# Queries moved into the stage of seven block products, with attention's operands passed through DRAM

## The chip, the cores and the metric

The kernel runs on one core of a Trainium2 chip. The metric is the device time of one execution in microseconds (us). A core has five engines with a queue of instructions each, which they work off in order: PE (TensorE, matmuls), DVE (VectorE), ACT (ScalarE), POOL (GpSimd) and SP (SyncE, which here only issues DMAs).

## What is computed

One layer of a hybrid streaming encoder on a stream of 16 meta tokens and 1024 frames, model width 1024, all in float32. Cut to the part around the change:

```python
h = h + 0.5 * swiglu(rmsnorm(h, ffn1_norm), ...)
u = rmsnorm(h, mix_norm)
(aq, ak, av, gq, gk, gv, gr, g_low, gate_a, gate_b) = split(u @ w_in)
ya = window_sink_attention(aq, ak, av, att_sinks)   # 8 heads of 64, 2 key heads, chunks of 64, 2 chunks back
yb = rmsnorm(gated_linear_attention(gq, gk, gv, log_sigmoid(g_low @ gla_gate_w + gla_gate_b) / 16)) * silu(gr)
h = h + (sigmoid(gate_a) * (ya @ w_branch_att) + sigmoid(gate_b) * (yb @ w_branch_gla)) @ w_out
h = h + 0.5 * swiglu(rmsnorm(h, ffn2_norm), ...)
return rmsnorm(h, final_norm)[:, 16:]
```

`aq` is 512 columns wide, `ak` and `av` 128 each, `gq` and `gk` 256 each, `gv` and `gr` 512 each, the two gates 1024 each.

## The kernel before

A float32 product is made from three reduced-precision ones: each operand is split into a high part (a cast, by ACT) and a low part (a subtraction, by DVE), and PE adds high × high, low × high and high × low. So 128 output columns over all of a 1024-row contraction and 512 frames are 8 × 3 = 24 matmuls, and over 1024 frames 48.

The projections `u @ w_in` are made in two forms. The plain form (`mm`, lines 96 to 98, tile `pj`) takes those 48 matmuls for each block of 128 columns; its weights come by one load (`raw`), one ACT cast (`whi`, L125) and one DVE subtraction (`wlo`, L126). The other form (`Group`, `product`, line 454) takes a pair of blocks of 128 columns and the two halves of the frames as a 2 × 2 block matrix, and makes it with seven block products of 12 matmuls instead of eight: 84 for a pair, where the plain form has 96. Its operands are sums and differences of weight blocks (`s`, L437, split into `wop` by L228 and L229). Four outputs come out of products 1, 4, 5 and 6 of a pair, each 128 × 512 (`gate_evac`).

In order of the program:

1. After the first feed-forward layer, `together` (tiles `pj` at L929, L930 and after) projects two blocks of `gk`, two of `gq` and the first of `gr` in the plain form, with the norm's scales made meanwhile.
2. The stage of seven products: the loop at L1104 over the 16 blocks of the two gates, in 8 pairs. The last four pairs also carry `decay`, the gate math of the linear attention, in ACT, DVE and SP. In this loop the order of PE, ACT and DVE is the order of the code; elsewhere a scheduler sets it.
3. Plain projections for the attention: `ak`, `av` and the four blocks of `aq` (`project_units`, a list of units, one for each chunk of frames: 512, 256 and 272 columns for those with meta tokens, `CH_T`, and two of 512 for those without, `CH_FR`). Their outputs are copied from PSUM into the layouts that the attention reads: keys, high parts in two tiles `kh`, low in `kl`; values `vcat`; queries `qs`, in two tiles that hold the high part of one key head beside the low part of it. `kh`, `kl` and `vcat` have 8 blocks of 16 meta columns, 2 zero columns and 128 frames. `build_bias`, on POOL, makes the table `bias` for the scores (L1164 to L1189), after the zero columns (L1160). Eight loads bring back the second half of the frames of four tiles of `u` (`uh`, `ul` from `b12_dram`).
4. The attention, 16 rounds (L1400): `turn` transposes the probabilities p of a chunk (`tp`), `scores` makes those of the next chunk (`sp`; softmax on DVE and ACT: the maximum `mx`, exps at L1299, reciprocal L1300, scaling L1302), `values` transposes a block of `vcat` (`vt`) and splits it into `vz`, and then PE runs what the round's entry of `slots` holds before `attend` multiplies p with the values (`po`). The slots are the projections of `gv` (L1348, two entries a block: the 512 chunk, then both others), of `gr` (L1351, six entries) and in the last two rounds two fill units each, parts of `ya @ w_branch_att` times the gate (`ga`, L1384). Two query units are held back and run after the first scores (L1398).
5. The remaining 12 fill units, the linear attention, `w_out`, the second feed-forward layer.

The stores of projected blocks of `gv` go out after a transposition one unit later (`late`, L903 to L912): PE transposes, DVE copies (`g`), SP stores.

The names of buffers are reused: `raw`, `whi` and `wlo` are the weights of any plain unit; a tile pool that is closed (`g7.close()`, L1120) gives its memory to later tiles, whose first writer then waits for the last reader of the old ones.

Of the kernel before, what the change touches and what calls it, by code (L numbers as in the profile page):

```python
# [8 lines left out]
F32 = mybir.dt.float32  # L9
# [26 lines left out]
def hybrid_kernel(  # L36
# [779 lines left out]
    plain_views = [cols_view(w_in, c) for c in (C_GK, C_GK + P, C_GQ, C_GQ + P, C_GR)]  # L816
# [64 lines left out]
    gr_dram = dram.tile([4, P, S], F32, name="gr_dram")  # L881
    b12_dram = dram.tile([4, 2, P, 512], F32, name="b12_dram")
# [6 lines left out]
    def ev_keep(dst, scale=None):  # L889
        def evac(ps, c0, n):  # L890
            g = ttile("g")
            nc.scalar.activation(g[:, 0:n], ps[:, 0:n], AF.Copy, scale=1.0 if scale is None else scale)
            nc.sync.dma_start(out=dst[:, c0:c0 + n], in_=g[:, 0:n])
        return evac

    def ev_tok(i):

        def evac(ps, c0, n):
# [4 lines left out]
            def turn():  # L903
# [3 lines left out]
                if c0 + n == T:  # L907
# [9 lines left out]
    plain_evac = [ev_keep(gk_dram[0]), ev_keep(gk_dram[1]), ev_keep(gq_dram[0], 0.125), ev_keep(gq_dram[1], 0.125),  # L917
                  ev_keep(gr_dram[0])]
# [53 lines left out]
    together([(2, CH_FR[1]), (3, CH_FR[1])])  # L972
# [38 lines left out]
    def gate_weights(m):  # L1011

        pair = []
        for i in range(2):
            pair.append(g8.ext_tile() if m % 4 else raw_tile())
            c = C_GA + (m + i) * P
            nc.sync.dma_start(out=pair[-1].rearrange("p (k m) -> p k m", k=KT),
                              in_=w_in[:, c:c + P].rearrange("(k p) m -> p k m", p=P))
        return Group(g8, *pair)

    def gate_out(m, i, c, x):
        if m < KT:
            nc.scalar.activation(x, x, AF.Sigmoid)
        nc.sync.dma_start(out=gates[m + i, :, c * 512:(c + 1) * 512], in_=x)
# [74 lines left out]
    group, follow = gate_weights(0), gate_weights(2)  # L1099
# [4 lines left out]
    for m in range(0, 16, 2):  # L1104
        others = [decay(*x) for x in pieces.pop(0)] if m >= KT else []
# [12 lines left out]
        group, follow = follow, gate_weights(m + 4) if m + 4 < 16 else None  # L1118
# [72 lines left out]
    def ev_k(ps, c0, n):  # L1191
        fr, p0 = min(n, S - c0) // P, c0 // P
        parts = [(lambda t, p: blocks(t)[p, p0:p0 + fr, MB:KB], lambda p: ps[p, 0:fr * P].rearrange("p (a b) -> p a b", b=P))]
        if c0 + n == T:
            parts.append((lambda t, p: blocks(t)[p, :, 0:NM], lambda p: ps[p, n - NM:n].unsqueeze(1).to_broadcast([p.stop - p.start, 8, NM])))
        lo_, hi_ = slice(0, 64), slice(64, P)
# [582 lines left out]
```

## Time and profile before

| | |
|---|---|
| time, median of 3 runs | 2018.44 us (2017.83 to 2019.83) |
| profiled execution: own time, span | 2016.82 us, 2015.1 us |
| granted PE clock | 0.997 |
| matmuls | 12060 |

Times inside the profile count from the start of the span. Stage 2 runs from 777.6 to 932.1, stage 3 from there to 1000, the attention's rounds to about 1140, and the remaining fill units and the linear attention to about 1235. In a row of groups the columns are line, engine, operation, tile written and tiles read, shapes, count, busy time, mean duration in ns, and the engine's idle time before these instructions with what ended it. In a row of a timeline they are start, duration, engine, line, operation, tiles, shapes, count, and in brackets the idle time before it and what ended it.

### The profile page before, as it was taken

To read this page: it belongs to the slowest core of one execution; us is meant where nothing else is said; L and a number is where in the kernel's file an instruction comes from. 1 tells how busy PE (TensorE), PEld (TensorE's weight loads), DVE (VectorE), ACT (ScalarE), POOL (GpSimd) and SP (SyncE) were. 2 spreads that over 40 slices of the span, in tenths; PEclk is the share of its full clock that TensorE was granted. 3 is DMA by queue.
4 is the path that set the end of the run, shared out by engine and by line. 5 is a ranking of instruction groups with operands and counts; after the bars stand their busy time and mean duration, and the time that the engine had idled before them with its cause. 6 is when DMAs were issued, how large, how long until landed. Compare 5 with 4: busy or idle time off the path is not lost.

```text
span 2015.1 us, 32030 instructions
## 1 busy us (share of the span) xinstructions
PE 1989.4 (99%) x12060; PEld 1767.3 (88%) x12060; DVE 1408.7 (70%) x2451; ACT 886.5 (44%) x1728; POOL 187.9 (9%) x223
## 2 busy tenths in 40 slices
PE   8999999999999999999999999999999999999998
PEld 7999999999999988888898768888888888878888
DVE  6976776675778785566466568469767767758875
ACT  5544444443322354465366445345444444442222
POOL 1000000002322000005000000110000000023212
PEclk9999999999999999999999999999999999999999
DMA  6243443349975343355212746741534534699722
GB/s 212 85 148 127 160 169 127 127 161 377 358 280 190 100 132 102 105 178 173 63 51 61 239 139 210 230 149 48 183 126 155 180 126 147 209 384 347 276 89 84
DMA packets 284619, 343.05 MB, mean 170 GB/s; under 512 B 26406, under 2 KB 192032, under 8 KB 284464
## 3 DMA queue, kind: packets, MB, share of 16 engines
q1 hardware_dynamic: 265376, 274.82, 41.2%
q10 hardware_dynamic: 17296, 61.29, 8.0%
q0 software_dynamic: 1792, 4.89, 0.7%
q8 instruction: 95, 1.56, 0.3%
q14 instruction: 60, 0.49, 0.1%
HBM read 220.66 MB, written 120.27 MB: 169 GB/s over the span
## 4 chain that ended last, share of the span: by engine, by line
PE 88%; DMA 5%; DVE 3%; issue 1%; ACT 1%; POOL 0%; SPq 0%; DVEq 0%; ACTq 0%; POOLq 0%
PE pb L454 35%; PE pd L454 17%; PE pa L454 9%; PE pj L96 2%; PE pj L97 2%; PE pj L98 2%; PE wo L96 1%; PE wo L97 1%; PE wo L98 1%; PE pd L841 1%; DMA tm<-f2mid 1%; PE pj L929 1%; PE pj L930 1%; PE pj L931 1%; DMA tm<-f1mid 1%
## 5 line engine op out<-in xcount | busy, mean ns | idle before, releaser
L454 PE MATMUL pb<-tt,wop 128*128 128x260 f32 (+1 forms) x2280 | 393.0, 326 | 0.0
L454 PEld LDWEIGHTS pb<-tt,wop 128*128 128x128 f32 x2280 | 339.8, 188 | 35.5
L229 DVE TENSOR_TENSOR wop<-s,wop 128x512 fp32r<-128x512 f32 x268 | 190.6, 714 | 119.6 <-ACT wop L228 119.1
L228 ACT CAST wop<-s 128x512 fp32r<-128x512 f32 x268 | 166.1, 621 | 234.2 <-PE pb L454 90.5
L454 PE MATMUL pb<-tm,wop 128*128 128x260 f32 (+1 forms) x1440 | 235.9, 319 | 5.5 <-ACT h L396 3.4
L454 PEld LDWEIGHTS pb<-tm,wop 128*128 128x128 f32 x1440 | 208.2, 189 | 25.3 <-ACT h L396 4.1
L228 ACT CAST wop<-raw 128x512 fp32r<-128x512 f32 x201 | 124.8, 622 | 221.6 <-PE pb L454 110.8
L229 DVE TENSOR_TENSOR wop<-raw,wop 128x512 fp32r<-128x512 f32 x201 | 144.7, 721 | 29.7 <-ACT wop L228 29.5
L454 PE MATMUL pd<-tt,wop 128*128 128x260 f32 (+1 forms) x792 | 138.2, 327 | 0.0
L454 PEld LDWEIGHTS pd<-tt,wop 128*128 128x128 f32 x792 | 118.9, 188 | 13.1
L454 PE MATMUL pd<-tm,wop 128*128 128x260 f32 (+1 forms) x720 | 119.1, 319 | 0.0
L341 DVE SCALAR_TENSOR_TENSOR h<-pb,h 128x520 f32<-128x520 f32 (+1 forms) x136 | 93.4, 692 | 36.5 <-PE pb L454 34.7
L454 PE MATMUL pb<-tb,wop 128*128 128x260 f32 (+1 forms) x696 | 115.3, 319 | 0.7 <-DVE m L742 0.7
L454 PE MATMUL pd<-tb,wop 128*128 128x260 f32 (+1 forms) x696 | 115.1, 319 | 0.0
L454 PE MATMUL pa<-tb,wop 128*128 128x260 f32 (+1 forms) x696 | 115.0, 318 | 0.0
L454 PEld LDWEIGHTS pd<-tm,wop 128*128 128x128 f32 x720 | 104.6, 189 | 9.4
L454 PEld LDWEIGHTS pb<-tb,wop 128*128 128x128 f32 x696 | 100.9, 188 | 10.1 <-ACT vec L87 0.8
L454 PEld LDWEIGHTS pa<-tb,wop 128*128 128x128 f32 x696 | 100.7, 188 | 9.3
L454 PEld LDWEIGHTS pd<-tb,wop 128*128 128x128 f32 x696 | 100.7, 188 | 9.3
L437 DVE TENSOR_TENSOR s<-raw 128x512 f32<-128x512 f32 x92 | 63.3, 688 | 53.6 <-DMA raw<-in_ffn_w_up 50.5
L341 DVE SCALAR_TENSOR_TENSOR h<-pd,h 128x520 f32<-128x520 f32 (+3 forms) x112 | 72.5, 654 | 31.5 <-PE pd L454 16.1
L437 POOL TENSOR_TENSOR s<-raw 128x512 f32<-128x512 f32 x28 | 37.5, 1340 | 602.8 <-DMA tm<-f2mid 425.0
(415 smaller groups left out, 3939.3 us busy)
## 6 DMA issues: line engine op xcount, KB each, us to landing
tm<-f1mid ACTq DMA_DIRECT2D x56, 520.0 KB, 6.3
tm<-f2mid ACTq DMA_DIRECT2D x56, 512.0 KB, 6.1
raw<-in_ffn_w_gate SPq DMA_DIRECT2D x42, 512.0 KB, 3.9
raw<-in_ffn_w_up SPq DMA_DIRECT2D x42, 512.0 KB, 3.9
raw<-in_ffn_w_down SPq DMA_DIRECT2D x80, 256.0 KB, 6.8
f2mid<-kh SPq DMA_DIRECT2D x70, 256.0 KB, 2.7
f2mid<-kl SPq DMA_DIRECT2D x70, 256.0 KB, 2.9
f1mid<-kh SPq DMA_DIRECT2D x63, 260.0 KB, 2.7
```

Of the source, the lines that this page charges most:

```text
L96: nc.tensor.matmul(ps, wh[k], xh[k], start=(k == 0), stop=False)
L97: nc.tensor.matmul(ps, wh[k], xl[k], start=False, stop=False)
L98: nc.tensor.matmul(ps, wl[k], xh[k], start=False, stop=(k == n - 1))
L228: nc.scalar.copy(x[:, 0:n], src)
L229: nc.vector.tensor_sub(x[:, n:2 * n], src, x[:, 0:n].bitcast(F32))
L341: nc.vector.scalar_tensor_tensor(hm, ps, 0.5, hm, op0=ALU.mult, op1=ALU.add)
L437: (eng.tensor_add if add else eng.tensor_sub)(a[s], a[x], a[y])
L454: nc.tensor.matmul(ps, y, z[:, s0:s0 + sn], start=(first and k == 0 and at == 0), stop=(at == 2 and k == len(cols) - 1), skip_group_check= ...
L841: nc.tensor.matmul(ps, y, x[:, c0 + s0:c0 + s0 + sn], start=(n == 0), stop=(n == 3 * LAST - 1), skip_group_check=True)
L929: nc.tensor.matmul(ps[:, 0:n], wh, xh, start=(k == 0), stop=False)
L930: nc.tensor.matmul(ps[:, 0:n], wh, xl, start=False, stop=False)
L931: nc.tensor.matmul(ps[:, 0:n], wl, xh, start=False, stop=(k == KT - 1))
```

## The change

The stage of seven products gets 11 pairs instead of 8: first the pair of `gq`, then two pairs of `aq`, then the gates. `ak` and `av` take the place of `gq` in `together`, in the plain form. The outputs that the attention needs are split into high and low at once and stored to DRAM (`ak_dram`, `av_dram`, `aq_dram`); after the stage SP loads them into `kh`, `kl`, `vcat` and `qs` in their final layout, and four POOL copies spread the meta columns. An output of `aq` (128 × 512) goes out as four stores of 64 × 8 × 64 numbers. The weights of the pairs alternate between two pools of tiles by the pair's number; with 11 pairs the last has those that the last but one had before. Between the stage and the first scores PE now has the 512-column chunks of the first three blocks of `gv`; `slots` holds what is left of `gv` in fewer entries, and fill units in the last four rounds (2, 1, 2 and 1). Ten fill units are left for later instead of 12.

```diff
--- before.py
+++ after.py
@@ -813,7 +813,7 @@
 
 
     wt = Weights([w_more, w_main, w_main, w_main], [r_main])
-    plain_views = [cols_view(w_in, c) for c in (C_GK, C_GK + P, C_GQ, C_GQ + P, C_GR)]
+    plain_views = [cols_view(w_in, c) for c in (C_GK, C_GK + P, C_AK, C_AV, C_GR)]
     raws = [wt.raw(v) for v in plain_views[0:2]]
     hw = [None] * 5
     dgs = {}
@@ -914,8 +917,13 @@
             late.append(turn)
         return evac
 
-    plain_evac = [ev_keep(gk_dram[0]), ev_keep(gk_dram[1]), ev_keep(gq_dram[0], 0.125), ev_keep(gq_dram[1], 0.125),
-                  ev_keep(gr_dram[0])]
+    def ev_ak(ps, c0, n):
+        hi, lo = [ttile(x, F32R)[:, 0:n] for x in ("hi", "lo")]
+        split(hi, lo, ps[:, 0:n])
+        for i, x in enumerate((hi, lo)):
+            nc.sync.dma_start(out=ak_dram[i, :, c0:c0 + n], in_=x.bitcast(F32))
+
+    plain_evac = [ev_keep(gk_dram[0]), ev_keep(gk_dram[1]), ev_ak, ev_keep(av_dram), ev_keep(gr_dram[0])]
 
     def together(pairs, hooks=()):
 
@@ -969,7 +977,7 @@
     together([(i, ch) for i in range(2) for ch in CH_T[1:]])
     hw[4] = ktiles(wt.cut(wt.raw(plain_views[4])))
     low_w = low_weights()
-    together([(2, CH_FR[1]), (3, CH_FR[1])])
+    together([(i, ch) for i in (2, 3) for ch in CH_T[1:]])
     ra.close()
     t_r = g7.enter_context(tc.tile_pool(name="tr", bufs=8, side="right"))
 
@@ -1008,20 +1016,44 @@
         nc.vector.tensor_sub(lo, b21[k], hi.bitcast(F32))
         g8.tops["T4"][k] = (hi, lo)
 
-    def gate_weights(m):
-
+    wq = w_in[:, C_AQ:C_AQ + 512].rearrange("(k p) (g i d) -> p k g i d", p=P, g=2, i=4)
+
+    PAIRS = [("q", 0)] + [("a", i) for i in (0, 2)] + [("g", m) for m in range(0, 16, 2)]
+
+    def gate_weights(at):
+
+        what, m = PAIRS[at]
         pair = []
         for i in range(2):
-            pair.append(g8.ext_tile() if m % 4 else raw_tile())
-            c = C_GA + (m + i) * P
-            nc.sync.dma_start(out=pair[-1].rearrange("p (k m) -> p k m", k=KT),
-                              in_=w_in[:, c:c + P].rearrange("(k p) m -> p k m", p=P))
+            pair.append(g8.ext_tile() if at % 2 else raw_tile())
+            if what == "a":
+                for g in range(2):
+                    nc.sync.dma_start(out=pair[-1].rearrange("p (k g d) -> p k g d", k=KT, g=2)[:, :, g, :], in_=wq[:, :, g, m + i, :])
+            else:
+                c = (C_GA if what == "g" else C_GQ) + (m + i) * P
+                nc.sync.dma_start(out=pair[-1].rearrange("p (k m) -> p k m", k=KT),
+                                  in_=w_in[:, c:c + P].rearrange("(k p) m -> p k m", p=P))
         return Group(g8, *pair)
 
-    def gate_out(m, i, c, x):
+    def gate_out(at, i, c, x):
+        what, m = PAIRS[at]
+        cols = slice(c * 512, (c + 1) * 512)
+        if what == "a":
+
+            hi, lo = [ttile(y, F32R) for y in ("hi", "lo")]
+            split(hi, lo, x)
+            for g, own, other in ((0, slice(0, 64), slice(64, P)), (1, slice(64, P), slice(0, 64))):
+                for rows, y in ((own, hi), (other, lo)):
+                    nc.sync.dma_start(out=aq_dram[g, rows, 8 * c:8 * c + 8, (m + i) * 64:(m + i) * 64 + 64],
+                                      in_=y[own, :].bitcast(F32).rearrange("p (a b) -> p a b", b=64))
+            return
+        if what == "q":
+            nc.scalar.activation(x, x, AF.Copy, scale=0.125)
+            nc.sync.dma_start(out=gq_dram[i, :, cols], in_=x)
+            return
         if m < KT:
             nc.scalar.activation(x, x, AF.Sigmoid)
-        nc.sync.dma_start(out=gates[m + i, :, c * 512:(c + 1) * 512], in_=x)
+        nc.sync.dma_start(out=gates[m + i, :, cols], in_=x)
 
     def gate_evac(m, i, ps, xs):
 
@@ -1096,13 +1128,13 @@
     pieces = [[(p, *CH_FR[0])] if c == 0 else [(p, *CH_FR[1]), (p, S, NM)] for p in range(2) for c in range(2)]
     AHEAD, cols = 2, [k * P for k in range(4)]
     g8.ring = [w_main] * 6
-    group, follow = gate_weights(0), gate_weights(2)
+    group, follow = gate_weights(0), gate_weights(1)
     made = [group.weights(i) for i in range(AHEAD)]
     group.sums(nc.vector)
     manual = tc.manual_schedule(engines={nc.scalar.engine, nc.vector.engine, nc.tensor.engine})
     manual.__enter__()
-    for m in range(0, 16, 2):
-        others = [decay(*x) for x in pieces.pop(0)] if m >= KT else []
+    for m in range(len(PAIRS)):
+        others = [decay(*x) for x in pieces.pop(0)] if len(PAIRS) - m <= 4 else []
         xs = {}
         for i in range(7):
             j = i + AHEAD
@@ -1115,7 +1147,7 @@
             gate_evac(m, i, group.product(i, made.pop(0), g8.tops, cols, 0, m), xs)
             for o in others:
                 next(o, None)
-        group, follow = follow, gate_weights(m + 4) if m + 4 < 16 else None
+        group, follow = follow, gate_weights(m + 2) if m + 2 < len(PAIRS) else None
     manual.__exit__(None, None, None)
     g7.close()
     r1.close()
@@ -1188,56 +1220,30 @@
 
     build_bias()
 
-    def ev_k(ps, c0, n):
...
-    def ev_v(ps, c0, n):
...
-    def ev_q(i):
...
-    wq = w_in[:, C_AQ:C_AQ + 512].rearrange("(k p) (g i d) -> p k g i d", p=P, g=2, i=4)
-
-    def q_units(i):
-        views = [(ALLROWS, lambda r, g=g: r.rearrange("p (k g d) -> p k g d", k=KT, g=2)[:, :, g, :], wq[:, :, g, i, :]) for g in range(2)]
-        return project_units(views, CH_FR, ev_q(i))
-
-    firsts = [project_units(cols_view(w_in, C_AK), CH_T, ev_k), project_units(cols_view(w_in, C_AV), CH_T, ev_v), q_units(0)]
-    for units in firsts:
-        units.pop(0)()
+
+    km = ap_.tile([P, 4, NM], F32, name="kmeta")
+    nc.sync.dma_start(out=blocks(vcat)[:, :, MB:KB], in_=av_dram[:, 0:S].rearrange("p (a b) -> p a b", b=P))
+    nc.sync.dma_start(out=km[:, 3, :], in_=av_dram[:, S:T])
+    lo_, hi_ = slice(0, 64), slice(64, P)
+    for to, j, i, rows, src in ((kh[0], 0, 0, lo_, lo_), (kh[0], 0, 0, hi_, lo_), (kh[1], 1, 0, lo_, hi_), (kh[1], 1, 0, hi_, hi_),
+                                (kl, 2, 1, ALLROWS, ALLROWS)):
+        nc.sync.dma_start(out=blocks(to)[rows, :, MB:KB].bitcast(F32), in_=ak_dram[i, src, 0:S].rearrange("p (a b) -> p a b", b=P))
+        nc.sync.dma_start(out=km[rows, j, :], in_=ak_dram[i, src, S:T])
+    for j, to in enumerate((kh[0], kh[1], kl, vcat)):
+        nc.gpsimd.tensor_copy(blocks(to)[:, :, 0:NM], km[:, j, :].unsqueeze(1).to_broadcast([P, 8, NM]))
+
+    def load_q(c):
+        for g in range(2):
+            nc.sync.dma_start(out=qs[g][:, 8 * c:8 * c + 8, :].bitcast(F32), in_=aq_dram[g, :, 8 * c:8 * c + 8, :])
+
+    v_units = [project_units(cols_view(w_in, C_GV + i * P), CH_T, ev_tok(i)) for i in range(4)]
+    for i in range(3):
+        v_units[i].pop(0)()
+    load_q(0)
     for k in range(4):
         for i, x in enumerate(halves_of(k, 1)):
             nc.sync.dma_start(out=x.bitcast(F32), in_=b12_dram[k, i])
-    for units in firsts:
-        for u in units:
-            u()
-    held = []
-    for i in range(1, 4):
-        units = q_units(i)
-        units[0]()
-        if i < 2:
-            units[1]()
-        else:
-            held.append(units[1])
+    load_q(1)
 
     def values(j):
 
@@ -1343,10 +1349,8 @@
             nc.vector.tensor_sub(u[own, 0:256], po[own, cols], qs[0][own, c, :].bitcast(F32))
         nc.vector.tensor_add(qs[1][:, c, :], u[:, 0:256], t[:, 0:256])
 
-    slots = []
-    for i in range(4):
-        us = project_units(cols_view(w_in, C_GV + i * P), CH_T, ev_tok(i))
-        slots += [us[0:1], us[1:3]]
+    vs = [u for units in v_units for u in units]
+    slots = [vs[0:2], vs[2:3], vs[3:5], vs[5:6], vs[6:7], vs[7:9]]
     for i in range(1, 4):
         slots += [[u] for u in project_units(cols_view(w_in, C_GR + i * P), CH_FR, ev_keep(gr_dram[i]))]
 
@@ -1390,13 +1394,11 @@
         views = [(slice(g * 64, g * 64 + 64), lambda r: r.rearrange("p (k m) -> p k m", k=4),
                   w_branch_att[g * 256:(g + 1) * 256, m0 * P:(m0 + 2) * P].rearrange("(i d) m -> d i m", d=64)) for g in range(2)]
         fill.append(branch_units(views, ya, m0, load_a, ev_a))
-    fill = fill[0][0:2] + fill[1][0:2] + fill[0][2:4] + fill[1][2:4] + fill[2] + fill[3]
-
-    slots += [[fill.pop(0), fill.pop(0)] for _ in range(2)]
+    fill = fill[0][0:2] + fill[1][0:2] + fill[2][0:2] + fill[0][2:4] + fill[1][2:4] + fill[2][2:4] + fill[3]
+
+    slots += [[fill.pop(0) for _ in range(n)] for n in (2, 1, 2, 1)]
     values(0)
     cur = scores(0)
-    held[0]()
-    held[1]()
     for c in range(16):
         nxt = None
         turn(cur)
```

PE's order at the end of the first plain units after the stage, where `values(0)` transposes `vcat`. The names end in buffer numbers; `pj_11075` is the second unit of `q`'s first block, `pj_11297` the second block's chunk of `gv`, `pj_11338` the third's. Before:

```order
L98 MATMUL pj_11075<-uh7_8385,wlo_11072 128x512
L1247 MATMUL vt_11104<-ident_75,vcat_10618 128x128
L1248 MATMUL vt_11104<-ident_75,vcat_10618 82x128
L1251 MATMUL vt_11104<-ident_75,vcat_10618 82x128
L1287 MATMUL sp_11117<-kh0_10615,qs0_10613 128x82
L1287 MATMUL sp_11118<-kh1_10616,qs1_10614 128x82
L96 MATMUL pj_11141<-uh0_8378,whi_11035 128x512
```

After:

```order
L98 MATMUL pj_11297<-uh7_8385,wlo_11294 128x512
L909 MATMUL vt_11322<-ident_75,v_11289 128x128 x4
L1253 MATMUL vt_11385<-ident_75,vcat_11155 128x128
L1254 MATMUL vt_11385<-ident_75,vcat_11155 82x128
L1257 MATMUL vt_11385<-ident_75,vcat_11155 82x128
L96 MATMUL pj_11338<-uh0_8378,whi_11334 128x512
```

The transposes of `vcat` stood behind all the projections of keys, values and most of the queries; now they stand behind two chunks of `gv`, and a third chunk and the first scores behind them.

POOL's order from the end of `build_bias`, whose last rows stand first; `tri` and `attb00` belong to the linear attention. Before:

```order
L1186 TENSOR_SCALAR bias_10622<-sink_10632 64x1
L1187 MEMSET bias_10622 64x1
L1433 MEMSET tri_12982 128x128
L1437 MEMSET attb00_12985 128x128
L1434 AFFINE_SELECT tri_12982<-tri_12982 128x128
```

After:

```order
L1218 TENSOR_SCALAR bias_11159<-sink_11169 64x1
L1219 MEMSET bias_11159 64x1
L1233 COPY vcat_11155<-kmeta_11241 128x8x16
L1233 CAST kh0_11152<-kmeta_11241 128x8x16
L1233 CAST kh1_11153<-kmeta_11241 128x8x16
L1233 CAST kl_11154<-kmeta_11241 128x8x16
```

The meta columns, which DVE and ACT wrote in `ev_v` and `ev_k`, are now written by POOL, behind all of the bias.

SP's order after, behind the stage's last store: the end of the loads of keys, then the first store of `gv` and the weights of its third block (`raw_11332`).

```order
L1230 DMA kl_11154<-ak_dram_8736 128x8x128
L1231 DMA kmeta_11241<-ak_dram_8736 128x16
L915 DMA gv_dram_8733<-g_11323 128x512
L117 DMA raw_11332<-in_w_in 128x8x128
L1237 DMA qs0_11150<-aq_dram_8738 128x2048
L1237 DMA qs1_11151<-aq_dram_8738 128x2048
L1245 DMA uh0_8378<-b12_dram_8739 128x512
```

In before the restores of `uh` and `ul` stood straight behind the stage's last store, and no store between them and the weights of the next plain units.

More of the change, by code (lines that the diff above doesn't have):

```diff
@@ L1189, in hybrid_kernel @@
     build_bias()
-    def ev_k(ps, c0, n):
[L1192 to L1196, printed above, removed]
-        for dst, src in parts:
-            for g, own, other in ((0, lo_, hi_), (1, hi_, lo_)):
-                nc.scalar.copy(dst(kh[g], own), src(own))
-                nc.scalar.copy(dst(kh[g], other), src(own))
-                nc.vector.tensor_sub(dst(kl, own), src(own), dst(kh[g], own).bitcast(F32))
```

18 lines of the change are left out of this document (5 added, 13 removed).

## The prediction

> **What bounds the kernel now.** I read the page first: the busy shares and the chain of work that ended last.
>
> ```profile
> span 2015.1 us, 32030 instructions
> PE 1989.4 (99%) x12060; PEld 1767.3 (88%) x12060; DVE 1408.7 (70%) x2451; ACT 886.5 (44%) x1728; POOL 187.9 (9%) x223
> PE 88%; DMA 5%; DVE 3%; issue 1%; ACT 1%; POOL 0%; SPq 0%; DVEq 0%; ACTq 0%; POOLq 0%
> ```
>
> PE is busy for all but 25.7 us, so every matmul taken away counts, and so does every microsecond for which PE newly waits. Next comes the price of a matmul: the chain inside the stage of seven products, then PE's timeline at the end of that stage.
>
> ```profile
> 777.83 2.77 PE pb L454 x12
> 780.60 2.72 PE pa L454 x12
> 794.20 5.44 PE pb L454 x24
> ```
>
> ```profile
> 926.29 0.39 PE L454 MATMUL pd<-uh,wop 128*128 128x512 f32 x1
> 929.24 0.47 PE L454 MATMUL pb<-uh,wop 128*128 128x512 f32 x1
> 932.08 0.39 PE L96 MATMUL pj<-uh,whi 128*128 128x512 f32 x1
> 937.52 0.39 PE L96 MATMUL pj<-uh,whi 128*128 128x512 f32 x1
> ```
>
> Twelve 512-column matmuls issue in 2.72 us (0.2267 each), and the 24 plain ones from 932.08 to 937.52 take 5.44, the same rate. The stage ends at 932.08; I call that moment E. Then the windows, one per stretch, which show where there is room:
>
> ```profile
> 815.80:834.90 19.10, 19.10 (x86) 15.82 (x85) 9.39 (x16) 8.56 (x15) 0.00 (x0) 1.00 0.37 112
> 932.00:945.00 13.00, 13.00 (x59) 10.74 (x58) 7.09 (x11) 3.97 (x6) 11.77 (x26) 1.00 1.04 330
> 945.00:1000.00 55.00, 55.00 (x291) 47.25 (x290) 21.66 (x44) 19.75 (x43) 13.96 (x36) 1.00 0.27 65
> 1000.00:1010.00 10.00, 9.40 (x56) 7.70 (x55) 5.99 (x20) 7.14 (x21) 0.00 (x0) 1.00 0.21 59
> 1010.00:1140.00 130.00, 129.77 (x837) 114.02 (x836) 90.38 (x308) 81.85 (x247) 0.00 (x0) 1.00 0.30 94
> ```
>
> Columns: length, then busy PE, PEld, DVE, ACT, POOL, the granted clock, the DMA share and GB/s. From E to 1000 PE never rests: 68 us of projections stand between the end of the stage and the first softmax. In the attention it loses 0.60 + 0.23 = 0.8 us. That cover is what the change spends.
>
> **The products.** Three pairs of column blocks (gq, and two of aq) go from the plain form (96 matmuls) to seven products (84): 36 fewer at 0.2267 = −8.2 us, all on the path. That ak and av take gq's place early moves work without changing it. A pair's extra output work (ACT 4, DVE 4 operations of 0.6 to 0.7 us) fits beside 19.1 us in which DVE is busy for 9.4 and ACT for 8.6: nothing, unless the stores hold the buffers (rival C). The copies of k and q that `ev_k`, `ev_v` and `ev_q` made lay under PE's 68 us: their removal is worth nothing.
>
> **POOL, in front of the first transposes.** After E there remain, before the first scores, only three 512-column chunks of values (16.3 us). Between the second and the third, PE's order has the transposes of `vcat`, and the second of these reads the meta columns, which are now written by a POOL copy at L1233. That copy stands in POOL's queue behind all of `build_bias`. POOL's timeline of before:
>
> ```profile
> 928.72 0.33 POOL L1160 CAST kh<-zero 128x16 fp32r<-128x16 f32 x2 [165.81 <-DVE wop L229]
> 929.13 0.20 POOL L1160 COPY vcat<-zero 128x16 f32<-128x16 f32 x1
> 937.75 1.58 POOL L1185 TENSOR_SCALAR bias<-nd 64x210 f32<-64x210 f32 x2
> 960.99 0.09 POOL L1187 MEMSET bias<- 64x1 f32 x1
> ```
>
> It starts at E − 3.4, when the stage's last readers free the memory, and runs without a gap to 961.08: 32.4 us. In before nothing early waited for it. In after the last pair's weights lie in other tiles, so DVE's reading of them should not be the releaser; the next is PE's product that ends at 926.3, E − 5.8. The queue is then through at E + 26.6, and the copy, 0.2 us for a small one above, a little longer for 128 columns, at E + 27.0. PE comes to L1254 at E + 10.9 + 0.6 (four transposes) = E + 11.5 and stands. Behind it in PE's queue is the third chunk; on ACT the cast of that chunk's weights stands behind the casts of `vz`, which need these transposes.
>
> ```profile
> 994.78 1.05 ACT L125 CAST whi<-raw 128x1024 fp32r<-128x1024 f32 x1 [1.40 <-issue]
> 995.86 1.23 DVE L126 TENSOR_TENSOR wlo<-raw,whi 128x1024 fp32r<-128x1024 f32 x1 [1.45 <-ACT whi L125]
> L1260 ACT CAST vz<-vt 128x128 fp32r<-128x128 f32 (+2 forms) x16 | 5.0, 314 | 16.9 <-DVE vz L1262 16.8
> ```
>
> Transposes 0.3, two casts 0.6, whi 1.05, wlo 1.23: the third matmul of the chunk issues at E + 30.2, and 22 × 0.2267 = 5.0 later it ends, E + 35.4 with a semaphore or two. Without a wait it would end at E + 17.0. Price: +18.4. Upper end: POOL released as before, +20.8. Lower end: POOL early, but the chunk's weights late, which SP sets:
>
> ```profile
> 919.57 0.43 SPq L1070 DMA_DIRECT2D q<-gq_dram  x1
> 929.12 0.32 SPq L1024 DMA_DIRECT2D gates<-x  x1
> 936.35 0.41 SPq L1078 DMA_DIRECT2D km_dram<-k  x1
> raw<-in_w_in SPq DMA_DIRECT2D x24, 512.0 KB, 4.0
> raw<-in_w_in SPq DMA_DIRECT2D x8, 256.0 KB, 4.1
> ```
>
> SP issues in order and stood from 919.57 to 929.12 for one result. It issues the last store of the stage at E + 4.3; then come 11 new loads at about 0.45, then the store of the first chunk of gv, which waits for DVE's copy behind the transposes (about E + 12.3), and only then the third chunk's weights: E + 12.8, landing 4.0 later, E + 16.8, plus 2.3 for whi and wlo and 5.0: E + 24.1, +7.1. This wait hides under POOL's now and is late next if POOL's goes. Four 1-MB loads of q and eight restores follow in that queue, with 18 us for them: nothing while PE stands.
>
> **The rounds of the attention.** With three chunks spent early, each remaining slot is shorter. PE's starts of the transposes of p, and DVE's end of the softmax:
>
> ```profile
> 1083.07 1.04 PE L1317 MATMUL tp<-ident,p 128*82 128x128 f32 x8
> 1091.41 1.36 PE L1317 MATMUL tp<-ident,p 128*128 128x128 f32 x8
> 1100.36 0.94 PE L1317 MATMUL tp<-ident,p 128*82 128x128 f32 x4
> 1090.69 0.18 DVE L1300 RECIPROCAL sm<-sm 128x4 f32<-128x4 f32 x1 [1.99 <-ACT p L1299]
> 1090.90 1.05 DVE L1302 TENSOR_SCALAR p<-p,sm 128x210 f32<-128x210 f32 x4
> 1099.88 1.05 DVE L1302 TENSOR_SCALAR p<-p,sm 128x210 f32<-128x210 f32 x4
> ```
>
> A round of 8.34 us with a slot of 24 matmuls (5.44) holds 2.90 of other PE work, and p is ready 1090.90 + 0.1 to 0.3 − 1083.07 = about 8.0 after the round's start. So a round needs a slot of 5.1, or PE waits. Round 1 has only a 256-column chunk (24 matmuls, an estimate at half of 0.2267: 2.7): 8.0 − 2.9 − 2.7 = 2.4, to 3.6 if the 1.23 us of wlo fall into the chain; I take 2.7. Round 3 has 272 columns, 2.9 by the same estimate: 2.2 (1.3 to 2.2, since their rate may be worse); I take 2.0. Round 13 has one fill unit of 12 matmuls (2.72): 2.4, and DVE can stand there for a load of gates, as it did later in before:
>
> ```profile
> 1143.66 0.69 DVE L1384 TENSOR_TENSOR ga<-br,ga 128x512 f32<-128x512 f32 x1 [4.00 <-DMA ga<-gates]
> 1140.00:1235.00 95.00, 90.10 (x530) 68.14 (x529) 58.05 (x139) 37.47 (x105) 1.15 (x7) 1.00 0.54 176
> ```
>
> I take 3.6 (1.9 to 6.4). Round 15, also one unit but no scores after it: 0.7 (0 to 2). Round 0, whose softmax was covered by two held query units and now is by seven matmuls: 1.0 (0.3 to 2). The stretch from 1140, which idles 4.9 us already, has two fill units fewer inside it: 0.7 (0 to 1.4). Together 10.7, bounds 5.5 and 14. What PE lost in before's attention (0.8) is part of these: −0.8.
>
> **Sum.** −8.2 + 18.4 + 10.7 − 0.8 = +20.1. The profiled execution took 2016.8 us (span 2015.1), so 2036.9; the median of the runs stands 1.6 above the profiled one: 2038.5. With the bounds: −8.2 + 7.1 + 5.5 − 0.8 = +3.6 (2022.0) to −8.2 + 20.8 + 14 − 0.8 = +25.8 (2044.2).
>
> **Rivals.** A: POOL's queue starts earlier than I read. It decides once the queue is through by E + 14, that is from a start before E − 18, nearly a whole pair earlier. Then the weights' wait of 7.1 is left: +8.8, 2027, down to 2022 with the rounds at their lower bounds. Against it: the first row of POOL above, an idle time of 165.81 us that ended at the stage's last pair.
>
> B, the other side: the count of matmuls alone decides, because the transposes of `vcat` find their columns written. One mechanism: the memory of `kh` and `vcat` is free before the last pair, so POOL starts before E − 21 and SP's loads, which wait for the same memory, leave the queue before the stage's last stores; chunk three then runs at E + 11.5, and the rounds wait as priced at their low end 5.5: −8.2 + 5.5 − 0.8 = −3.5 (2014.9); it is faster by up to 9.0 (2009) if they too are covered. For it only that the names of the freed tiles differ; against it the same row.
>
> C: the stores of q are slow. Each of the eight outputs of the two q pairs goes out as four stores of 64 × 8 pieces of 256 bytes, 4 MB in all, from two tiles out of a ring of four. Loads of 256-byte pieces took 4.1 us for 256 KB, where 512 KB in longer pieces took 4.0: half the rate. With four issues (1.8) and 4.1 to land, an output holds its tiles for some 6 us, and outputs 2 to 4 of a pair come 2.72 apart: ACT can wait 1 to 3.5 us per pair, against a lead of two products (5.44) in the weights. So nothing, unless a store takes over 8 us; then up to 3 us a pair: +6, 2044.5. The Trainium skill, "DMA: Bandwidth & Descriptors", section Specifications, wants 512 bytes or more for a transfer at line rate and says that less makes the engine read, modify and write; the rows of the loads agree on the halving, and no row of before shows such a store.
>
> **Chances.** The forecast 0.70, A 0.12, B 0.08, C 0.10. About 0.2% (4 us) is what a measurement can tell from no change. Faster by more: most of B and nothing else, 0.07. Within: the rest of B and the lower end of A, 0.05. Slower: 0.88. The range from A's lower end to C's time, 2022 to 2045, leaves out B and a little at the top.
>
> **What the profile after will show.** Right: PE idle of 16 to 20 us just after the stage, named for POOL's L1233 or the ACT and DVE steps behind it; POOL's bias running without a gap into the copies; weights of the third value chunk landing before PE needs them; the three new pairs at 19.0 us each, no wait in them; transposes of p 8 us apart with PE waiting on p in rounds 1, 3 and 13; 36 fewer matmuls. The forecast falls if POOL's first cast of `kh` starts more than 18 us before E, if PE's wait there is under 8 us, or if a q pair takes over 20 us.

## The result and the profile after

The changed kernel takes 2041.59 us (median of 4 runs, 2041.08 to 2044.02), the kernel before 2018.13 beside it. The ratio is 1.0118, with a 95% interval of 1.0106 to 1.0129: about 24 us slower, with 36 matmuls fewer. The forecast was 2038.5. The head of the page:

```profile
span 2039.3 us, 32102 instructions
PE 1990.4 (98%) x12024; PEld 1767.2 (87%) x12024; DVE 1419.2 (70%) x2470; ACT 890.9 (44%) x1737; POOL 189.1 (9%) x227
```

PE's busy time has not fallen with the number of matmuls (1989.4 before), a first sign that some of them run slower. Three of PE's waits are new or have grown, from the list of waits (total, times, longest):

```profile
PE vt L1254 <- POOL vcat L1233: 15.3, 1, 15.3
PE tp L1323 <- DVE p L1308: 7.6, 5, 2.4
PE pj L96 <- ACT whi L125: 2.5, 1, 2.5
```

Before, PE waited 0.8 us in all for p at the transposes, and the other two waits were not on its list. POOL's timeline around the end of the stage, E, which is now at 991.33:

```profile
985.83 1.00 POOL L1192 CAST kh<-zero 128x16 fp32r<-128x16 f32 x2 [145.61 <-PE pb L454]
...
1017.70 0.09 POOL L1219 MEMSET bias<- 64x1 f32 x1
1017.86 0.29 POOL L1233 COPY vcat<-kmeta 128x128 f32<-128x128 f32 x1
```

POOL starts at E − 5.5, released by a PE product (forecast: E − 5.8, by a PE product), works through the bias without a gap, and makes the copy for which PE stands at E + 26.5. PE's timeline there:

```profile
991.33 0.39 PE L96 MATMUL pj<-uh,whi 128*128 128x512 f32 x1
...
1002.65 0.27 PE L1253 MATMUL vt<-ident,vcat 128*128 128x128 f32 x1
1018.21 0.44 PE L1254 MATMUL vt<-ident,vcat 128*82 128x128 f32 x1 [15.29 <-POOL vcat L1233]
1018.44 0.42 PE L1257 MATMUL vt<-ident,vcat 128*82 128x128 f32 x1
1021.32 0.80 PE L96 MATMUL pj<-uh,whi 128*128 128x512 f32 x1 [2.46 <-ACT whi L125]
...
1028.94 0.60 PE L909 MATMUL vt<-ident,v 128*128 128x128 f32 x4
```

The third value chunk runs from 1021.32 to 1028.94: 7.62 us for 24 matmuls that take 5.44 elsewhere. The windows tell why (the column before the last two is the granted clock):

```profile
1018.20:1021.30 3.10, 0.65 (x2) 0.21 (x2) 0.71 (x2) 2.02 (x5) 0.68 (x3) 0.50 0.02 6
1021.30:1023.50 2.20, 2.14 (x4) 1.32 (x5) 1.23 (x1) 0.00 (x0) 0.00 (x0) 0.50 0.00 0
1025.30:1028.90 3.60, 3.60 (x17) 2.94 (x16) 0.00 (x0) 0.00 (x0) 0.00 (x0) 1.00 0.00 0
```

PE comes out of the wait at half its clock and keeps that until about 1025. The same is to be seen after waits of 1.9 to 2.4 us in the attention's rounds 1, 3 and 13:

```profile
1049.41 1.94 PE L1323 MATMUL tp<-ident,p 128*128 128x128 f32 x8 [2.31 <-DVE p L1308]
1068.69 1.69 PE L1323 MATMUL tp<-ident,p 128*128 128x128 f32 x8 [1.86 <-DVE p L1308]
1158.51 1.97 PE L1323 MATMUL tp<-ident,p 128*128 128x128 f32 x8 [2.39 <-DVE p L1308]
1047.00:1049.40 2.40, 0.10 (x1) 0.02 (x1) 0.90 (x4) 2.39 (x11) 0.00 (x0) 0.94 0.61 164
1049.40:1052.00 2.60, 2.59 (x12) 2.42 (x12) 1.63 (x6) 1.75 (x5) 0.00 (x0) 0.50 0.33 104
```

Eight transposes that took 1.04 us before take 1.69 to 1.97 here. After the wait of 1.86 the clock falls a little later, at 1069.6, and stays at half until 1073.0.

Put together from the two timelines, the 24.2 us by which the span grew lie like this: the stage of seven products starts 2.1 later (777.67 to 779.79), 1.3 of it already at the first projection of `together` (712.55 to 713.82); it is 57.1 longer (three pairs at 19.04); from its end to the first transposes of p it is 25.9 shorter (68.1 to 42.2); the rounds to the last transposes take 134.9 in both; and what follows is 9.1 shorter.

### The profile page after: what moved, and what is told of

The parts are those of the page before. It is cut to its first block, busy times and chain, and to the rows that moved or that the text cites. A ratio compares the mean times of both kernels' runs of the same rounds, so it can differ in the third digit from the quotient of the medians.

```text
span 2039.3 us, 32102 instructions
## 1 busy us (share of the span) xinstructions
PE 1990.4 (98%) x12024; PEld 1767.2 (87%) x12024; DVE 1419.2 (70%) x2470; ACT 890.9 (44%) x1737; POOL 189.1 (9%) x227
## 5 line engine op out<-in xcount | busy, mean ns | idle before, releaser
L454 PE MATMUL pb<-tt,wop 128*128 128x260 f32 (+1 forms) x2352 | 410.4, 328 | 0.6 <-ACT g L314 0.6
L454 PEld LDWEIGHTS pb<-tt,wop 128*128 128x128 f32 x2352 | 353.2, 188 | 39.1 <-ACT g L314 0.8
L229 DVE TENSOR_TENSOR wop<-s,wop 128x512 fp32r<-128x512 f32 x280 | 199.0, 714 | 119.1 <-ACT wop L228 118.4
L228 ACT CAST wop<-s 128x512 fp32r<-128x512 f32 x280 | 173.6, 621 | 236.1 <-PE pb L454 96.9
L454 PEld LDWEIGHTS pb<-tm,wop 128*128 128x128 f32 x1440 | 208.2, 189 | 26.5 <-ACT h L396 4.7
L228 ACT CAST wop<-raw 128x512 fp32r<-128x512 f32 x210 | 130.3, 622 | 222.9 <-PE pb L454 111.6
L229 DVE TENSOR_TENSOR wop<-raw,wop 128x512 fp32r<-128x512 f32 x210 | 149.8, 715 | 39.4 <-ACT wop L228 39.2
L454 PE MATMUL pd<-tt,wop 128*128 128x260 f32 (+1 forms) x828 | 146.8, 330 | 0.0
L454 PEld LDWEIGHTS pd<-tt,wop 128*128 128x128 f32 x828 | 125.6, 188 | 14.5
```

The lines of the kernel that those rows point to most:

```text
L228: nc.scalar.copy(x[:, 0:n], src)
L229: nc.vector.tensor_sub(x[:, n:2 * n], src, x[:, 0:n].bitcast(F32))
L454: nc.tensor.matmul(ps, y, z[:, s0:s0 + sn], start=(first and k == 0 and at == 0), stop=(at == 2 and k == len(cols) - 1), skip_group_check= ...
```

## The experiments

All edits are to the changed kernel, unless another is named. The kernel before varied from 2014.5 to 2024.6 in these series, so ratios are given with their intervals, and sizes under 0.2% are read from the traces.

**1. The meta columns by DVE.**

```diff
-        nc.gpsimd.tensor_copy(blocks(to)[:, :, 0:NM], km[:, j, :]...)
+        nc.vector.tensor_copy(blocks(to)[:, :, 0:NM], km[:, j, :]...)
```

> The four copies of the meta columns are made by DVE instead of POOL; nothing else changes. Theory (POOL's queue): the 15.3 us for which PE waits for POOL at the transposes of vcat go. Next late are the third value chunk's weights (loaded at about E + 12.8, landing E + 16.8, used from E + 18, and PE at half clock for some 3.5 us again) and then the bias, with which POOL is through at E + 26.9: the first transposes of p come at E + 31 to E + 33 instead of E + 42.2, so 9 to 11 us less than the changed kernel's 2041.6: 2031 to 2033. Rival (the loads of the meta columns in SP's queue are what is late): the wait stays, now named for DVE, and the time falls by less than 3 us.

Measured: 2030.61 us, ratio 1.0059 (1.0044 to 1.0074). The wait for POOL is gone from the list, and the next two rows of the timeline are the ones that were forecast (E is 992.33 here):

```profile
1011.24 0.80 PE L96 MATMUL pj<-uh,whi 128*128 128x512 f32 x1 [7.09 <-ACT whi L125]
1023.60 0.48 PE L1323 MATMUL tp<-ident,p 128*82 128x128 f32 x2 [0.81 <-DVE p L1308]
```

A wait of 7.1 us for the weights, and first transposes of p at E + 31.3. POOL's queue is shown as the cause of the stall: four copies of 0.3 us on another engine bring the first transposes of p 10.9 us forward (E + 42.2 to E + 31.3); by the ratios (1.0118 to 1.0059) it is some 12.

**2. The weights of the third chunk earlier.** All three value units get their `raw` loads by hand; the third is asked for after the first unit instead of in its own.

> As e1_meta_dve, and the weights of the third value chunk are loaded before the first store of gv instead of behind it. Theory: the third chunk runs straight behind the second (no wait, no half clock there, end at about E + 17), but the first softmax then stands for the bias until POOL is through at E + 26.9, so hardly anything is gained over e1_meta_dve: 0 to 2 us, 2030 to 2032. Rival (the bias is not late, since the softmax reads only its first half): 7 us less than e1_meta_dve, about 2025.

Measured: 2031.43 us, ratio 1.0060 (1.0045 to 1.0075): no gain, as forecast, but not for the reason given. The scheduler put the load ahead of the store and left it behind the eleven loads of keys, so the wait for the weights went from 7.09 only to 6.60. E is 990.03 in this trace:

```profile
1001.61 0.43 SPq L117 DMA_DIRECT2D raw<-in_w_in  x1
1008.44 0.79 PE L96 MATMUL pj<-uh,whi 128*128 128x512 f32 x1 [6.60 <-ACT whi L125]
```

So it doesn't tell the bias from the weights. The next kernel does.

**3. The weights ahead of the loads of keys.** In the program the loads of `kh`, `kl` and `kmeta` move behind the third chunk's `raw`, and the first loads of the queries follow them.

> As e1_meta_dve (meta columns by DVE), with the weights of all three value chunks loaded ahead of the loads of keys, and the first queries right behind these. Theory: the third chunk then runs without a wait (until E + 17), and the bias, with which POOL is through only at E + 26.9, is what is late: the softmax stands for it, first transposes of p at E + 29 to E + 30.5 (e1: E + 31.3): 1 to 2 us less than e1, 2028.5 to 2030. Rival (the softmax of the first chunk does not need the end of the bias): 7 to 9 us less than e1, 2022.

Measured: 2029.20 us, ratio 1.0046 (1.0028 to 1.0064); first transposes of p at 1019.62, E + 29.3 (E is 990.29), as expected. The wait for the weights is gone; in its place PE stands for the queries' load:

```profile
1011.63 0.62 PE L1298 MATMUL sp<-kh,qs 128*128 128x82 f32 x2 [3.60 <-DMA qs<-aq_dram]
```

The time came out right and the wait that was named (the bias) wrong: the softmax of the first chunk starts on DVE at 1012.97, while POOL is at the bias until 1017.25, so it doesn't need the bias's end. PE stands 4.5 us for loads (these 3.60, and 0.86 for a restore), and from 1011.4 to 1021.6, past the first transposes of p, its granted clock is 0.50, which adds to the delay.

**4. The even half of the bias by DVE.** On top of experiment 3:

```diff
-                    nc.gpsimd.tensor_scalar(b, nd[rows, :], ...)
+                    (nc.vector if par == 0 else nc.gpsimd).tensor_scalar(b, nd[rows, :], ...)
```

> As e2b_load_order, and the half of the bias multiplications that belongs to even chunks is made by DVE, so that POOL is through earlier (about E + 20). Theory: with POOL's queue, the weights and the bias all out of the way the first transposes of p come at E + 21 to E + 24; the waits in the rounds stay: 8 to 10 us less than e1, 2020 to 2023. Rival (the loads of keys and queries, 3.3 MB behind the stage, are late next): first transposes of p not before E + 27, 2026.

A miss: 2032.83 us, ratio 1.0066 (1.0051 to 1.0082). The interval overlaps that of experiment 3, but the first transposes of p come at E + 33.0 (E is 990.32), 3.7 later than there. DVE's timeline, SP's and PE's:

```profile
992.55 1.61 DVE L1217 TENSOR_SCALAR bias<-nd 64x210 f32<-64x210 f32 x5 [3.35 <-POOL nd L1212]
994.09 0.68 DVE L1067 TENSOR_TENSOR x<-pd,x 128x512 f32<-128x512 f32 x1
989.23 0.38 SPq L117 DMA_DIRECT2D raw<-in_w_in  x1
994.79 0.32 SPq L1056 DMA_DIRECT2D gates<-x  x1
999.77 0.80 PE L98 MATMUL pj<-uh,wlo 128*128 128x512 f32 x1 [3.40 <-DVE wlo L126]
```

The scheduler put the new work ahead of the stage's last outputs on DVE. DVE waits there 3.35 us for POOL; the output `x` comes late, SP's store of it too, and with SP's queue all loads of keys and queries, by 4 to 5 us. POOL was through earlier (at 1012.2), and nothing came of it.

**5. The rounds filled evenly.** Only the slots are changed:

```diff
-    slots = [vs[0:2], vs[2:3], vs[3:5], vs[5:6], vs[6:7], vs[7:9]]
+    slots = [vs[0:2], vs[2:4], vs[4:6], vs[6:7], vs[7:9]]
-    slots += [[fill.pop(0) for _ in range(n)] for n in (2, 1, 2, 1)]
+    slots += [[fill.pop(0) for _ in range(n)] for n in (2, 2, 2, 2, 0)]
```

> The changed kernel with the attention's rounds filled evenly: the chunks of gv in five entries (two chunks each, 512 alone), six of gr, then two fill units in each of rounds 11 to 14 and none in round 15 (the first branch's weights are loaded twice). The stall behind the stage stays. Theory: the waits of 2.3, 1.9, 0.2 and 2.4 us on the softmax go, and with the three long ones the half clock behind them, about 1.3 us each; round 15 gets up to 2.5 back: 7 to 9 us less, 2033 to 2035. Rival (a lower clock in the records costs nothing by itself): the waits alone, less 2.5: about 2037.5.

Measured: 2038.90 us, ratio 1.0093 (1.0071 to 1.0114). By the ratios that is about 5 us less than the changed kernel, but the two intervals overlap, and from the first transposes of p to the end of the span the trace gains only 1.5 (1005.8 to 1004.3); both are short of the 7 to 9 that I expected. The waits of rounds 1 and 3 are gone. That of round 13 is still there:

```profile
1157.65 0.69 DVE L1388 TENSOR_TENSOR ga<-br,ga 128x512 f32<-128x512 f32 x1 [4.27 <-DMA ga<-gates]
1158.94 1.46 PE L1323 MATMUL tp<-ident,p 128*128 128x128 f32 x8 [2.19 <-DVE p L1308]
```

A full slot doesn't help where DVE stands 4.27 us for a load of gates with the softmax behind it. The empty round 15 cost 2.4 us of waits for the parts of p.

**6. Useless work in the gaps.**

```diff
+        if c in (1, 3, 13):
+            idle = bank("pj")
+            for k in range(12):
+                nc.tensor.matmul(idle, u_hi[k % 4][:, 0:P], u_hi[4][:, 0:512], start=(k == 0), stop=(k == 11), ...)
```

> The changed kernel with twelve useless matmuls (2.72 us) added in each of rounds 1, 3 and 13, into a bank that nobody reads; they add work and take none away. Theory (an idle time of about 2 us halves PE's clock for some 3 us): PE works through the waits, the clock stays up, and each of the three rounds loses its 1.3 us of half clock but gains 0.3 to 0.9 us by which the dummies outlast the wait: 2 to 3 us less, 2038.5 to 2039.5. Rival (the clock follows from the idle time in the record only): 1 to 1.6 us more, 2043.

Measured: 2036.77 us, ratio 1.0089 (1.0074 to 1.0105): faster than without the 36 dummy matmuls. Here the place of the half clock above reads:

```profile
1048.80 1.12 PE L1323 MATMUL tp<-ident,p 128*128 128x128 f32 x8
1049.40:1052.00 2.60, 2.60 (x24) 2.38 (x23) 1.42 (x3) 2.49 (x7) 0.00 (x0) 1.00 0.02 6
```

The clock stays at 1.00. The round behind, from these transposes to the next, takes 9.80 us, where the changed kernel took 11.06: 1.26 us of half clock for a wait of 2.3. From the first transposes of p to the end of the span, 2.85 us are gained (1005.8 to 1002.95), within the 2 to 3 expected, and all of it in the rounds: those behind the three waits are 1.26, 1.76 and 1.22 shorter, those that hold the dummies 0.28, 0.62 and 0.49 longer.

**7. gq alone in the stage.** Nine pairs; the queries of the attention are projected plainly into `qs` behind the stage, slots and fill units as before the change; ak and av still go through DRAM.

> One part of the change alone: gq in the stage of seven products (9 pairs), ak and av in its early place and through DRAM; the queries of the attention are projected plainly behind the stage as before (8 units, 43.5 us of cover), and slots and fill units are those of before. POOL makes the meta columns as in the changed kernel. Theory: 12 matmuls fewer (2.7 us) and nothing late, since the transposes of vcat stand at E + 33, behind POOL's E + 27: 1.5 to 3 us faster than before, 2015.5 to 2017. Rival (passing the operands through DRAM costs by itself): no faster than before, or slower.

A miss: 2029.34 us, ratio 1.0053 (1.0036 to 1.0071).

```profile
963.73 0.46 SPq L117 DMA_DIRECT2D raw<-in_w_in  x1
970.02 0.79 PE L96 MATMUL pj<-uh,whi 128*128 128x512 f32 x1 [11.37 <-ACT whi L125]
```

The bias was covered, as I had argued, but the second unit's weights stand behind the eleven loads of keys in SP's queue. I had read that queue for the changed kernel's third chunk only.

**8. The same with the weights first.** Three units' weights ahead of the loads of keys, meta columns by DVE.

> As e6_gq_only, where PE stood 11.4 us for the weights of the second query unit behind SP's loads of keys: here the weights of the first three query units are loaded ahead of them, the third unit's first chunk is run early, and DVE makes the meta columns. Theory (that wait and the half clock behind it were the whole loss): the wait goes and 12 matmuls fewer remain: 1 to 3 us faster than before, ratio 0.9985 to 0.9995. Rival (the stretch behind the stage is bound by its transfers whatever their order): no better than 1.003.

Measured: 2022.35 us, ratio 1.0013 (1.0001 to 1.0024). The wait of 11.4 is gone; left are waits for the weights' low part and the restores:

```profile
965.72 0.50 PE L98 MATMUL pj<-uh,wlo 128*128 128x512 f32 x1 [0.66 <-DVE wlo L126]
973.53 0.49 PE L96 MATMUL pj<-uh,whi 128*128 128x512 f32 x1 [2.53 <-DMA uh<-b_dram]
```

Between the two theories: most of the loss was the order, but what is saved (2.7 us) is eaten by later transfers. The trace can't say by how much, since it is of the slowest of the eleven runs: its stage starts 2.2 us later than in the trace of before, 1.3 of it already at the first projection of `together`, and the part behind the last transposes of p, which has the work of before, takes 3.1 longer.

**9. Bias half by DVE, weights first, and the rounds filled evenly.** Experiment 4, with five entries of gv, four of gr, four of two fill units, two of gr, and an empty one.

> As e3b_cover, and the rounds filled evenly: five entries of gv, four of gr, four of two fill units (the weights of the first two branches are loaded twice), two of gr, and none in round 15. Theory: all that the changed kernel waits for is gone but for round 0, round 15 (2.4 us) and what is left behind the stage (3 to 6 us): 5 to 8 us less than e3b, 2013 to 2017, so as fast as before or a little faster with all 36 matmuls saved. Rival (late loads of gates hold DVE in the fill rounds as in e4's round 13): no more than 3 us less than e3b.

Measured: 2027.61 us, ratio 1.0044 (1.0029 to 1.0058), 5 us less than experiment 4, as the change of the rounds alone should give; 10 to 15 above the forecast, since experiment 4 had missed by that. PE waits 0.8 us for p in all, against 7.6 in the changed kernel; at the end of the stage the 3.40 us on DVE stand as above.

**10. The bias half by ACT.** Experiment 9 with `nc.scalar.activation(b, nd[rows, :], AF.Copy, scale=...)` for the even half.

> As e7_all, with the half of the bias multiplications made by ACT, which has nothing to do there, instead of DVE, where they stood ahead of the stage's last results and of the weights' low parts (3.4 us of wait at PE, 5.5 us of delay to SP's loads). Theory: that wait goes and the loads come 5 us earlier, so that the first scores wait for their queries up to 3 us only: 5 to 7 us less than e7_all, 2020 to 2022.5. Rival (the transfers, not the order, set the first scores): less than 3 us gained.

Measured: 2025.81 us, ratio 1.0034 (1.0022 to 1.0047). The intervals overlap; from E to the first transposes of p 2.1 us are gained (33.6 to 31.5), the size that the rival named, but not for its reason. ACT now does what DVE did in experiment 4: it stands for POOL in front of the copy of the stage's last product. SP's loads of the queries come only 1.1 us earlier by E (at E + 17.0), not 5, and PE's wait for them grew:

```profile
993.88 3.19 ACT L1218 ACTIVATE bias<-nd 64x210 f32<-64x210 f32 x8 [3.79 <-POOL nd L1212]
998.05 0.58 ACT L1062 COPY x<-pb 128x512 f32<-128x512 f32 x1
1015.68 0.39 PE L1301 MATMUL sp<-kh,qs 128*128 128x82 f32 x2 [4.24 <-DMA qs<-aq_dram]
```

**11. Half of the queries.** Ten pairs: gq and one pair of aq in the stage, the other pair plain behind it (three chunks, then one held behind the first scores), one chunk of gv, 13 full slots and three rounds of two fill units.

> The change with half the queries: gq and one pair of aq in the stage of seven products (10 pairs), the other pair projected plainly behind it (4 chunks, 21.8 us of cover, one of them held behind the first scores), one chunk of gv there instead of three, weights ahead of the loads of keys, meta columns by DVE; 13 slots of gv and gr and three rounds of two fill units, none short. Theory: 24 matmuls fewer (5.4 us), bias and loads covered to E + 27, at most 2 to 3 us of waits new: 2 to 4 us faster than before, ratio 0.998 to 0.999. Rival (2 MB of queries read back in pieces and 2 MB of keys in front of the restores saturate the DMA engines and hold the first scores for over 5 us): same as before or slower.

Measured: 2016.89 us, ratio 0.9991 (0.9982 to 1.0000). It is the only version that reaches the time of before, and the interval ends at no change; PE waits 1.55 us for a restore and 1.8 for the softmax. The kernel saves 5.4 us of matmuls and keeps about 2 (0 to 3.6 by the interval).

**12. The same with half of the bias by ACT.**

> As e8_half_queries, with the bias multiplications of even chunks made by ACT, so that POOL is through with the bias some 6 us earlier. Theory: the 1.8 us for which the first transposes of p waited for the softmax behind the bias go: 1 to 2 us less than e8, ratio to before 0.998 to 0.999. Rival (that wait is the distance from scores to softmax, not the bias): the same as e8.

A miss again: 2022.02 us, ratio 1.0020 (1.0011 to 1.0029). ACT, SP and PE:

```profile
976.66 3.21 ACT L1218 ACTIVATE bias<-nd 64x210 f32<-64x210 f32 x8 [4.55 <-POOL nd L1212]
979.89 0.59 ACT L1062 COPY x<-pb 128x512 f32<-128x512 f32 x1
975.12 0.51 SPq L1098 DMA_DIRECT2D km_dram<-e  x1
980.51 0.32 SPq L1056 DMA_DIRECT2D gates<-x  x1
997.56 0.80 PE L96 MATMUL pj<-uh,whi 128*128 128x512 f32 x1 [6.11 <-DMA uh<-b_dram]
```

ACT stands 4.55 us for POOL in front of the copy of the stage's last product; the store of that stands at the head of SP's queue, and every load behind it, down to the restores, is 5 us late. It is experiments 4 and 10 over again.

## Why the prediction was right, point by point

The direction and the place were right: a wait at L1254 on POOL's copy behind the whole bias, shown by experiment 1, and inside it the weights' wait, which experiment 1 uncovered. That 7.1 was forecast there and 7.09 measured is chance: the forecast was for the chunk's end, E + 24.1, which came at E + 26.7 in experiment 1, since PE was at half clock again; 7.09 is PE's idle time. POOL's start at the release by a PE product came as read, within 0.3 us, and the reason given for it holds: with ten pairs (experiment 11), where the last pair has the other pool of tiles, POOL starts at E − 3.4, released by DVE as before.

- Matmuls, −8.2: 36 fewer in the page, and the three pairs at 19.04 without a wait.
- The stall, forecast +18.4. From E to the third chunk's end are 37.6 us, 17.0 without waits: 20.6, at the upper bound. 15.3 + 2.5 are the waits; the rest, 2.9, is mostly the half clock (the chunk alone took 2.2 longer), which the prediction did not have.
- The rounds, forecast 2.7, 2.0, 3.6, 0.7 for rounds 1, 3, 13, 15 and 1.0 for round 0. Measured: 2.31, 1.86, 2.39, and 0.81 for round 0; round 15 has no wait on p. In round 1 the subtraction `wlo` does stand in the softmax chain, and in round 13 the product with the gates, as read from the order; in round 13 that cost some 0.6, since the exps ended only when it started (1157.3). So these terms were too high by some 2.5 us, and 4.2 us of half clock (1.26, 1.76 and 1.22 by experiment 6), not in the sum, more than made up for it.
- The start of the stage came 2.1 us later, where I had costed the exchange of gq for ak and av at nothing. Only 0.85 of that lies between the first projection of `together` and the stage (65.12 before, 65.97 after, 65.92 to 65.96 in the twelve others), where ak and av come in three chunks instead of two; part of this should come back behind the stage, where these chunks no longer stand. The other 1.3 were there at the first projection, in code that the change doesn't touch: the other traces of changed kernels start `together` at 712.51 to 714.91, three of them within 0.06 us of the single trace of before. So this part is variation from run to run and no cost of the change.
- Behind the last transposes of p 9.1 us were gained: three fill units fewer (one in round 15, two later) at 2.72 are 8.2. The 1.4 of new waits that had been taken for round 15 and that part did not come.

So the waits and their places were understood, and what each costs PE was not: the half clock behind them, about 2.9 us behind the stage and 4.2 in the rounds, has no term in the sum. That the time came out within 3 us is luck in part. The waits that were set too high cancel some 4 us of it, and the 1.6 us that were added because the median of before stood above its profiled execution did not come again (2041.62 profiled, median 2041.59): from span to span the growth is 24.2, where 20.1 was forecast.

Of the rivals, A and B fall with POOL's start at E − 5.5. C falls too: the stores of 64 × 8 pieces of 256 bytes took 2.6 to 2.8 us to land in the median, far from 8, and the two pairs with them had no wait. The window is that of the first:

```profile
aq_dram<-hi SPq DMA_DIRECT2D x15, 128.0 KB, 2.6
798.80:817.90 19.10, 19.10 (x86) 15.82 (x85) 11.07 (x18) 8.57 (x15) 0.00 (x0) 1.00 0.55 126
```

So the penalty on short pieces that the Trainium skill names in "DMA: Bandwidth & Descriptors", section Specifications, cost PE nothing at this load (126 GB/s were moved). Whether these stores pay it is open: the stores of 128 KB of `ak` in longer pieces took 1.7 us in the same trace, other stores of that size up to 2.6.

The prediction named one thing "late next", the weights. There were three in a row, each within a few microseconds of the other: POOL's copy, the weights, and the 2 MB of queries. Experiment 3 took the first two away and met the third. The bias, which I took for the next one, was not late (experiment 3); experiments 4, 9, 10 and 12 moved half of it all the same, and in each the engine that took it stood for POOL and held back the stage's last store. What stays open is how much of the last 10 us behind the stage belongs to the transfers themselves and how much to the half clock behind the waits for them: a kernel with less to load in that stretch and the full change was not run. Experiment 11, which loads half of the queries, points to the transfers.

## What to carry to other kernels

A stage that hides nothing itself may hide much for others: the 68 us of plain projections covered POOL's 32 us of bias and the loads of weights and of `u`, and a change that makes them cheaper elsewhere has to find that cover again. Read each queue up to the first instruction that the critical engine needs, past everything that stands ahead of it: a copy of 0.3 us behind 32 us of others cost 15, and work that was moved to an "idle" engine but waited there, in front of a result that SP had to store, delayed every load behind that store by 4 to 5. A wait of about 2 us on PE can cost more than its length: the three here cost another 1.2 to 1.8 us each in half clock.

## What the runs showed of the hardware

PE's granted clock fell to 0.50 about the end of a wait of 2.3 us and stayed there for 3.4 us; after one of 1.86 it fell too, 0.9 us after PE had gone on; after one of 1.2 us it was 1.00 (before, at 1144). Thirty-six useless matmuls that filled three such waits made the kernel faster by 2.85 us in the trace.

The length of a wait is not all that counts. In the changed kernel's trace the clock falls at 1008.15 (in the stall), 1049.11, 1069.59 and 1158.34 (rounds 1, 3 and 13); these moments lie 12, 6 and 26 times 3.41 us apart. The three short times at half clock last 3.41 us each, the one from 1008.15 to 1025.22 five times that. So in this trace the clock changes on a grid of 3.41 us, and how a wait lies on that grid should matter beside its length. The wait of round 3 is as long in experiment 3 as in the changed kernel, and there no half clock follows (first row and window: changed kernel; last two: experiment 3):

```profile
1068.69 1.69 PE L1323 MATMUL tp<-ident,p 128*128 128x128 f32 x8 [1.86 <-DVE p L1308]
1069.59:1073.00 3.41, 3.41 (x17) 2.86 (x15) 3.14 (x6) 2.56 (x7) 0.00 (x0) 0.50 0.26 81
1056.76 1.37 PE L1328 MATMUL tp<-ident,p 128*128 128x128 f32 x8 [1.89 <-DVE p L1313]
1056.70:1062.00 5.30, 5.24 (x31) 4.28 (x32) 5.03 (x15) 3.42 (x10) 0.00 (x0) 1.00 0.28 81
```

How much work in a step of the grid keeps the clock up was not tested.

The Trainium skill, "TensorE: Matmul & The Clock Gate", Part 1, says that PE falls to half its clock after an idle window of about 3.4 us and comes back after as long a time of work. The way back agrees with the trace (1021.3 to 1025.3), and so does the length of the step; the fall came here after shorter idle times, 1.9 to 2.4 us, and what was measured decides for this kernel.
